# The first stage of a decoder layer: activations loaded channel-major and scaled by a row of rstd, instead of normalised and transposed

## The chip, the cores and the metric

The kernel runs on one core of one Trainium2 chip. The metric is the device time of one execution in microseconds (us), median of three runs; lower is better. Six queues of work matter: TensorE (PE, with its weight loads as PEld), VectorE (DVE), ScalarE (ACT), GpSimd (POOL), SyncE (SP), which issues nearly all loads, and the 16 DMA engines that carry them.

## The reference, cut to what matters

One layer: a normalised input is projected once for three token mixers, the mixers are merged, and a mixture of experts follows. The change touches only the two lines that begin it.

```
h    = rmsnorm(x, g_mix)                  # x (512, 1024): y = x * rsqrt(mean(x*x, -1) + eps) * g
proj = einsum('bsd,dc->bsc', h, w_in)
...
kv   = einsum('bmd,dc->bmc', rmsnorm(mem, g_mem), w_mem_kv)   # mem (256, 1024), w (1024, 1024)
k_m, v_m = split(kv, 2)
k_m  = rmsnorm(k_m per head, g_km)
```

## The kernel before, in words

Every fp32 product is made of three fast ones: each operand is split into a rounded high part and a rest, and `mm3` (L156 to L159) adds high by high, high by rest and rest by high. The split of a weight chunk is one cast on ACT (`wh`, L127) and one subtraction on DVE (`wl`, L128); that of an activation is one ACT instruction and one DVE instruction (`evac_split`, L153 and L154).

The first stage, "mem kv", does two things at once. It multiplies the memory tokens by the eight chunks of `w_mem_kv`, k = 0 to 7, each 128 rows of the contraction and 512 KB: per chunk two halves of tokens (m) by two halves of columns (n), so four groups of three products of 512 columns, twelve in all, summed over the chunks in four PSUM banks (`kvp`). And it makes `hh`/`hl`, the split and normalised x with channels on partitions, which all later projections read. For that x is loaded token-major in four tiles (L255), its squares are summed per token (L223 on ACT, L225 on DVE), `rsqrt` (L144) runs a scale on DVE and a power on POOL for each tile, DVE multiplies the tile by it in two halves (`xn`, L265), PE transposes 32 blocks of 128 by 128 (`transpose_x`, L248), and each of the eight results is split out of PSUM.

The order in which each engine works is fixed when the program is built: a scheduler lays out the instructions of each engine in one list, and the engine takes them in that order, each waiting for its inputs. SP issues the loads in list order too. The weight chunks go through a ring of three buffers (tag "w"), so the load of chunk k + 3 is issued only after the DVE split of chunk k. Behind the eight chunks come the first projections, "conv" (L330 on, products at L314), which need all of `hh` and `hl`; the scheduler puts the small transposes of the normalised keys `kn` (L301) among their first products.

Much later, in the stage "w_o", x is loaded once more, channel-major, from `xt` (L798), and the experts' weights are fetched ahead by SP (`fetch`, L772) into every buffer that the earlier stages give back.

Of the kernel before, what the change touches and what calls it, by code (L numbers as in the profile page):

```python
# [8 lines left out]
F32 = mybir.dt.float32  # L9
F32R = mybir.dt.float32r  # L10
# [10 lines left out]
P = 128  # L21
# [68 lines left out]
def build(nc, tc, I, O, dbg=None):  # L90
    V, A, G, T, SY = nc.vector, nc.scalar, nc.gpsimd, nc.tensor, nc.sync
    es = ExitStack()
    with es:
# [25 lines left out]
        tri16 = cpool.tile([P, 2 * P], BF16, name="tri16")  # L119
        nhalf = cpool.tile([P, 16], F32, name="nhalf")  # L120
        G.memset(nhalf, -0.5)

        def small(name, n, dt=F32, tag="small", bufs=16):
            return cpool.tile([P, n], dt, name=name, tag=tag, bufs=bufs)
# [57 lines left out]
        def h_pairs(name):  # L182

            hi, lo = [], []
            for k in range(KD):
                if k >= 3:
                    x2 = hp.tile([P, 1024], F32R, name=f"{name}{k}", tag="hw" if k < 6 else "hx", bufs=3 if k < 6 else 2)
                    hi.append(x2[:, 0:512])
                    lo.append(x2[:, 512:1024])
                    continue  # L190
                tags = ("xh", "xl") if k < 2 else ("th", "ah")
                hi.append(hp.tile([P, 512], F32R, name=f"{name}h{k}", tag=tags[0], bufs=2 if k < 2 else 1))
                lo.append(hp.tile([P, 512], F32R, name=f"{name}l{k}", tag=tags[1], bufs=2 if k < 2 else 1))
            return hi, lo
# [31 lines left out]


        mark("mem kv")
        kv_raw = [raw_w("kv", 0)]
        mx = [hp.tile([P, D], F32, name=f"m{i}", tag=("hx", "hw")[i // 2], bufs=2 + i // 2) for i in range(4)]  # L230
        SY.dma_start(mx[0], I["memt"][0])
        kv_raw.append(raw_w("kv", 1))
        SY.dma_start(mx[1], I["memt"][1])
        SY.dma_start(csg[:, 0:P], I["cst"][:, C_KEEP:C_KEEP + P])
        kv_raw.append(raw_w("kv", 2))
# [16 lines left out]
        xn, rm = [], []  # L252
        for k in range(KD):
            if k < NT:
                SY.dma_start(xt0[k], I["x"][k])  # L255
            elif k < NT + 2:
                SY.dma_start(mx[k - 2], I["mem"][k - NT])
            if k == 3:
                for t in range(NT):
                    ss = small("ss", 1)  # L260
                    sum_sq(ss, xt0[t], t != 1, "y")
                    rsqrt(ss, ss, 1.0 / D, EPS)
                    for i in range(2):
                        xn.append(g2("B", f"xn{t}{i}"))
# [3 lines left out]
            wh, wl = split_w(kv_raw[k] if k < RING else raw_w("kv", k))  # L268
            for m in range(2):
                o = (k % 2) * 256 + m * P  # L270
                ah, al = mh[k // 2][:, o:o + P], ml[k // 2][:, o:o + P]
                for n in range(2):
# [521 lines left out]
        x_v = I["xt"].rearrange("k p n -> p k n")  # L794
        X = []
        for c in range(KD // 2):
            xt = rp.tile([P, 2, S], F32, name=f"xr{c}", tag="xc", bufs=2)
            SY.dma_start(xt, x_v[:, 2 * c:2 * c + 2])  # L798
            X.append(xt)
        wo_raw = [raw_w("wo", c) for c in range(KD)]  # L800
        gB = eat("wg", "gB")
# [476 lines left out]
def layout(x, mem, g_mix, w_in, b_gate, g_qa, g_ka, g_idx_k, conv_w, conv_b, ln_g, ln_b, g_mem, w_mem_kv,  # L1278
# [45 lines left out]
    def row(a):  # L1324
# [11 lines left out]
    return dict(x=x.reshape(NT, P, D), xt=np.ascontiguousarray(x.T).reshape(KD, P, S), mem=mem.reshape(2, P, D),  # L1336
                memt=np.ascontiguousarray(mem.T.reshape(2, 4, P, 256).transpose(0, 2, 1, 3)).reshape(2, P, D), wp=wp, we=we, sm=sm,
                gf=f(g_ffn), cst=constants())

# [34 lines left out]
```

## Time and profile before

| | |
|---|---|
| median of 3 runs | 776.18 us (774.14 to 776.66) |
| profiled execution | 777.4 us, its span 775.6 us |
| PE busy | 714.2 us (92% of the span) |
| DVE, ACT, POOL busy | 478.5, 266.0, 94.8 us |
| loads and stores | 161.13 MB, mean 208 GB/s |

The span is what the profile's times are counted in; about 2 us of the execution lie around it. Busy shares are means over stages that have different limits, so the first 60 us, where the change lies, have to be read by themselves, in the timeline and in windows of 2 us.

### The profile page before, as it was taken

Reading aid. Unit: us, or ns where it says so; the run is one execution under the profiler, and the core shown is the slowest. Engines: PE = TensorE matmul, PEld = TensorE weight load, DVE = VectorE, ACT = ScalarE, POOL = GpSimd, SP = SyncE. Lnnn points to the kernel's source line nnn. Section 1 sums busy time; section 2 is a strip of 40 time slices with the busy share of each in tenths; the row PEclk is TensorE's granted clock in tenths of the full one; section 3 lists DMA queues with packets and bytes.
Section 4 is the critical chain, followed back from the end, with each engine's and each line's share of the span. In section 5 each row is a group of like instructions: output and inputs, shape, how many; then the busy total and the mean of one; then the engine's idle time right before and its main releaser. Section 6 shows DMA issues by size and latency. Waiting matters only on the chain. (4 is left out here: it accounts for less than half of the span.)

```text
span 775.6 us, 10017 instructions
## 1 busy us (share of the span) xinstructions
PE 714.2 (92%) x3434; PEld 477.7 (62%) x3434; DVE 478.5 (62%) x1086; ACT 266.0 (34%) x502; POOL 94.8 (12%) x82
## 2 busy tenths in 40 slices
PE   6999999999999999999998999749999999789882
PEld 4778888887878778887776888633333333233220
DVE  5879989999999999999985844371211212111100
ACT  6732255365632466246774322101111111000100
POOL 1010010022000140000000000121226421100011
PEclk9999999999999999999999999858999999999997
DMA  9632311213223223220314799958999999999982
GB/s 357 219 123 81 93 72 55 81 56 109 82 81 90 75 81 102 89 82 27 109 55 190 247 368 336 365 208 299 394 385 363 353 379 377 373 382 388 396 336 52
DMA packets 56684, 161.13 MB, mean 208 GB/s; under 512 B 9508, under 2 KB 17956, under 8 KB 56624
## 3 DMA queue, kind: packets, MB, share of 16 engines
q1 hardware_dynamic: 41264, 147.21, 51.7%
q0 software_dynamic: 6624, 8.46, 4.8%
q10 hardware_dynamic: 8736, 4.73, 2.0%
q8 instruction: 29, 0.48, 0.2%
q14 instruction: 31, 0.25, 0.1%
HBM read 162.93 MB, written 13.11 MB: 227 GB/s over the span
## 5 line engine op out<-in xcount | busy, mean ns | idle before, releaser
L1143 PE MATMUL up<-we,xt 128*64 128x512 f32 x544 | 142.2, 611 | 4.3 <-DMA we<-in_we 4.2
L127 ACT CAST wh<-w 128x1024 fp32r<-128x1024 f32 (+2 forms) x75 | 78.3, 1046 | 88.1 <-PE proj L314 22.4
L128 DVE TENSOR_TENSOR wl<-w,wh 128x1024 fp32r<-128x1024 f32 (+2 forms) x75 | 91.0, 1214 | 10.5 <-ACT wh L127 8.6
L1143 PEld LDWEIGHTS up<-we,xt 128*64 128x64 f32 x544 | 39.6, 139 | 80.0 <-issue 60.5
L328 DVE SCALAR_TENSOR_TENSOR y<-u,conv_wh,y 128x512 f32<-128x512 f32 x120 | 84.2, 745 | 0.3
L1133 DVE COPY y<-dn 128x512 f32<-128x512 f32 x17 | 11.8, 692 | 109.9 <-PE dn L1157 109.9
L1157 PE MATMUL dn<-we,acth 128*64 128x512 f32 x272 | 74.7, 610 | 0.8 <-issue 0.6
L314 PE MATMUL gate<-h,wh 128*128 128x512 f32 x240 | 67.8, 397 | 0.0
L1132 ACT COPY y<-dn 128x512 f32<-128x512 f32 x17 | 10.0, 586 | 123.6 <-PE dn L1157 70.0
L1157 PEld LDWEIGHTS dn<-we,acth 128*64 128x64 f32 x272 | 24.2, 139 | 44.9 <-issue 36.7
L314 PEld LDWEIGHTS gate<-h,wh 128*128 128x128 f32 x240 | 44.4, 188 | 9.6
L1134 POOL DMA_INDIRECT out<-y,midx x16 | 25.4, 1585 | 137.2 <-DVE y L1133 109.3
L314 PE MATMUL gate<-h,wl 128*128 128x512 f32 x120 | 34.6, 399 | 0.0
L314 PE MATMUL mm<-h,wh 128*128 128x512 f32 x120 | 32.7, 396 | 0.0
L1151 DVE COPY acth<-atr 128x256 f32<-128x256 f32 x17 | 7.2, 425 | 39.3 <-PE atr L1149 33.1
L1115 ACT COPY xt<-xtr 128x512 f32<-128x512 f32 x17 | 9.9, 584 | 61.0 <-PE xtr L1114 61.0
L422 ACT ACTIVATE gt<-gate,bgate 128x512 f32<-128x512 f32 x24 | 16.5, 686 | 39.7 <-PE gate L314 39.5
L1126 DVE SCALAR_TENSOR_TENSOR acts<-up,mwt,acts 128x256 f32<-128x256 f32 x16 | 7.7, 484 | 31.7 <-ACT acts L1125 30.2
L604 DVE MAX8 v<-score 128x8 f32<-128x256 f32 (+2 forms) x48 | 26.6, 558 | 0.8
L605 DVE MATCH_REPLACE8 score<-v,score 128x256 f32<-128x256 f32 (+2 forms) x48 | 26.0, 543 | 0.0
L314 PEld LDWEIGHTS gate<-h,wl 128*128 128x128 f32 x120 | 22.4, 187 | 5.5 <-issue 0.5
L314 PEld LDWEIGHTS mm<-h,wh 128*128 128x128 f32 x120 | 22.4, 187 | 5.2
(396 smaller groups left out, 1441.2 us busy)
## 6 DMA issues: line engine op xcount, KB each, us to landing
we<-in_we SPq DMA_DIRECT2D x192, 512.0 KB
w<-in_wp SPq DMA_DIRECT2D x75, 512.0 KB
x<-in_x SPq DMA_DIRECT2D x4, 512.0 KB
xr<-in_xt SPq DMA_DIRECT2D x4, 512.0 KB
out<-x1t ACTq DMA_DIRECT2D x8, 256.0 KB
h2d<-x1t ACTq DMA_DIRECT2D x8, 256.0 KB
m<-in_memt SPq DMA_DIRECT2D x2, 512.0 KB
m<-in_mem SPq DMA_DIRECT2D x2, 512.0 KB
```

Of the source, the lines that this page charges most:

```text
L127: A.copy(wh, w)
L128: V.tensor_sub(wl, w, wh.bitcast(F32))
L314: T.matmul(ps, a[:, k * P:(k + 1) * P], b[k], start=(a is wh and b is rh and k == 0), stop=(b is rl and k == n - 1))
L328: V.scalar_tensor_tensor(Y[c], U[c][:, j:j + S], w, Y[c], op0=ALU.mult, op1=ALU.add)
L422: A.activation(t, ps, AF.Tanh, scale=0.5, bias=bgate[:, b * 8 + c:b * 8 + c + 1])
L604: V.max(v8, sel[t])
L605: V.match_replace(sel[t], v8, sel[t], GONE)
L1132: A.copy(y[:, 0:512], yp[0])
L1133: V.tensor_copy(y[:, 512:1024], yp[1])
L1134: G.indirect_dma_start(out=O["out"], out_offset=bass.IndirectOffsetOnAxis(ap=ix[:, col:col + 1], axis=0), in_=y, in_offset=None, bounds_ch ...
L1143: T.matmul(ps[h * CAP:(h + 1) * CAP], xt[k // 4][:, o + h * CAP:o + (h + 1) * CAP], ws[h][:, i * 512:(i + 1) * 512], start=(k == 0), stop= ...
L1157: T.matmul(yp[n][h * CAP:(h + 1) * CAP], at[:, f * P + h * CAP:f * P + (h + 1) * CAP], ws[h][:, n * 512:(n + 1) * 512], start=(f == 0), st ...
```

## The change

`xt`, the channel-major copy of x that the host lays out, is stored as four contiguous blocks of two channel groups (so L798 now reads 4 KB in one piece per partition), and it is loaded in the first stage too, as eight tiles `xc` of 256 KB. The token-major x is still loaded, for the squares alone. The four columns of sums go through one `rsqrt`. PE then multiplies the broadcast column by the identity, four times, which gives one PSUM tile in which every partition holds the row of 512 factors; ACT copies it to SBUF (`rows`). Even tiles are multiplied by the row on DVE, which reads it from PSUM, odd tiles on POOL, which reads the copy. The eight splits then read `xc` in SBUF.

Beside that, ten products of a zeroed tile that nobody reads stand ahead of PE's work; chunk 0 and the first memory tile are loaded and split in halves; the loop over a chunk's products has columns outside and tokens inside; and the load of chunk 2 goes ahead of that of the constants.

```diff
+        warm = cpool.tile([P, P], F32, name="warm")
+        V.memset(warm, 0.0)
...
+        junk = trt()
+        for _ in range(10):
+            T.matmul(junk[:, 0:P], warm, warm, start=True, stop=True)
+        for i in range(2):
+            SY.dma_start(w0[:, i * 512:(i + 1) * 512], I["wp"][W_KEYS.index(("kv", 0)), :, i * 512:(i + 1) * 512])
+            SY.dma_start(mx[0][:, i * 512:(i + 1) * 512], I["memt"][0, :, i * 512:(i + 1) * 512])
...
-        def transpose_x():
+        xc = [g2("B", f"xc{k}") for k in range(KD)]
+        def norm_x():
+            row = trt()
+            for t in range(NT):
+                T.matmul(row[:, t * P:(t + 1) * P], rx[:, t:t + 1].to_broadcast([P, P]), ident, start=True, stop=True)
+            rows = g2("ms", "row")
+            A.copy(rows, row)
             for k in range(KD):
-                ps = (trt if k % 2 == 0 else sct)()
-                for t in range(NT):
-                    T.transpose(ps[:, t * P:(t + 1) * P], xn[2 * t + k // 4][:, (k % 4) * P:(k % 4 + 1) * P], ident)
-                evac_split(hh[k], hl[k], ps, Q["g_mix"][:, k:k + 1])
+                if k % 2:
+                    G.tensor_mul(xc[k], xc[k], rows)
+                else:
+                    V.tensor_mul(xc[k], xc[k], row)
+                evac_split(hh[k], hl[k], xc[k], Q["g_mix"][:, k:k + 1])
...
         for k in range(KD):
...
+            if 2 <= k < 6:
+                for i in range(2):
+                    n = 2 * (k - 2) + i
+                    SY.dma_start(xc[n], x_v[n // 2, :, i * 512:(i + 1) * 512])
             if k == 3:
                 for t in range(NT):
-                    ss = small("ss", 1)
-                    sum_sq(ss, xt0[t], t != 1, "y")
-                    rsqrt(ss, ss, 1.0 / D, EPS)
-                    for i in range(2):
-                        xn.append(g2("B", f"xn{t}{i}"))
-                        V.tensor_scalar_mul(xn[-1], xt0[t][:, i * 512:(i + 1) * 512], ss)
+                    sum_sq(rx[:, t:t + 1], xt0[t], t != 1, "y")
+                rsqrt(rx, rx, 1.0 / D, EPS)
             if k == 5:
-                transpose_x()
+                norm_x()
```

The lists that the scheduler makes differ from the start of the program to the first projection; after it they are the same on every engine. Three places matter. SP's list after the first chunks, before (w is a weight chunk, x a token-major tile, m_104 and m_105 the token-major memory):

```order
L255 DMA x_72<-in_x 128x1024
L255 DMA x_73<-in_x 128x1024
L132 DMA w<-in_wp 128x1024
L257 DMA m_104<-in_mem 128x1024
L132 DMA w<-in_wp 128x1024
L257 DMA m_105<-in_mem 128x1024
L132 DMA w<-in_wp 128x1024 x3
```

and with the change:

```order
L271 DMA x_72<-in_x 128x1024
L277 DMA xc_163<-in_xt 128x512
L277 DMA xc_164<-in_xt 128x512
L271 DMA x_73<-in_x 128x1024
L277 DMA xc_165<-in_xt 128x512
L277 DMA xc_166<-in_xt 128x512
L134 DMA w<-in_wp 128x1024
L273 DMA m_116<-in_mem 128x1024
L277 DMA xc_167<-in_xt 128x512
L277 DMA xc_168<-in_xt 128x512
L134 DMA w<-in_wp 128x1024
```

Two `xc` tiles now stand ahead of the last x tile, four ahead of chunk 3, six ahead of chunk 4 and eight ahead of chunk 5.

DVE's list from the split of chunk 4 to that of chunk 6, before (h_143 to h_147 are tiles 3 to 7 of the activations):

```order
L128 TENSOR_TENSOR wl<-w,wh 128x1024
L154 SCALAR_TENSOR_TENSOR h_143<-sc,sm,h_143 128x512
L145 TENSOR_SCALAR rm<-rm 128x1 x2
L154 SCALAR_TENSOR_TENSOR h_144<-tr,sm,h_144 128x512
L128 TENSOR_TENSOR wl<-w,wh 128x1024
L154 SCALAR_TENSOR_TENSOR h_145<-sc,sm,h_145 128x512
L154 SCALAR_TENSOR_TENSOR h_146<-tr,sm,h_146 128x512
L154 SCALAR_TENSOR_TENSOR h_147<-sc,sm,h_147 128x512
L128 TENSOR_TENSOR wl<-w,wh 128x1024 x2
```

and with the change (h_158 to h_162 are the same five tiles, xc_169 is tile 6):

```order
L130 TENSOR_TENSOR wl<-w,wh 128x1024
L156 SCALAR_TENSOR_TENSOR h_158<-xc_166,sm,h_158 128x512
L156 SCALAR_TENSOR_TENSOR h_159<-xc_167,sm,h_159 128x512
L264 TENSOR_TENSOR xc_169<-xc_169,tr 128x512
L156 SCALAR_TENSOR_TENSOR h_160<-xc_168,sm,h_160 128x512
L147 TENSOR_SCALAR rm<-rm 128x1 x2
L156 SCALAR_TENSOR_TENSOR h_161<-xc_169,sm,h_161 128x512
L156 SCALAR_TENSOR_TENSOR h_162<-xc_170,sm,h_162 128x512
L130 TENSOR_TENSOR wl<-w,wh 128x1024 x3
```

The split of chunk 5 stood between tiles 4 and 5 and stands behind all of them now.

POOL's list, before, from its first power to the keys':

```order
L146 TENSOR_TENSOR ss<-ss,nhalf 128x1 x4
L146 TENSOR_TENSOR rm<-rm,nhalf 128x1 x2
L146 TENSOR_TENSOR kss<-kss,nhalf 128x4 x2
L146 TENSOR_TENSOR rsm<-rsm,nhalf 128x4 x4
L146 TENSOR_TENSOR kss_1550<-kss_1550,nhalf 128x3
```

and with the change:

```order
L148 TENSOR_TENSOR rx<-rx,nhalf 128x4
L262 TENSOR_TENSOR xc_164<-xc_164,row 128x512
L262 TENSOR_TENSOR xc_166<-xc_166,row 128x512
L262 TENSOR_TENSOR xc_168<-xc_168,row 128x512
L262 TENSOR_TENSOR xc_170<-xc_170,row 128x512
L148 TENSOR_TENSOR rm<-rm,nhalf 128x1 x2
```

One power of four columns stands for four of one, and four products of 512 columns follow it.

## Rows read from the trace of the kernel before

**Rows 1.** Windows: PE, PEld, DVE, ACT, POOL busy (count), granted clock, DMA share, GB/s.
```profile
440.00:500.00 60.00, 58.75 (x313) 49.63 (x312) 24.80 (x37) 16.59 (x24) 1.92 (x2) 0.98 0.99 348
...
560.00:650.00 90.00, 89.30 (x446) 33.41 (x446) 17.19 (x31) 12.70 (x23) 31.78 (x28) 1.00 1.02 370
```
**Rows 2.** Chain that ended last: start, length, what.
```profile
742.06 12.44 DMA we<-in_we
```
**Rows 3.** Waits of SP's queue from 380 us on: total, times, longest.
```profile
SPq L798 <- PE pva L706: 0.3, 1, 0.3
```
**Rows 4.** Windows of the first stage, columns as in rows 1.
```profile
18.00:20.00 2.00, 0.77 (x5) 0.53 (x5) 1.15 (x4) 0.00 (x0) 0.70 (x2) 1.00 1.03 410
...
22.00:24.00 2.00, 2.00 (x7) 1.53 (x7) 1.79 (x3) 2.00 (x4) 0.00 (x0) 0.59 0.59 123
```
**Rows 5.** Timeline of PE: start, length, instruction, wait before it.
```profile
16.25 0.40 PE L159 MATMUL kv<-wh,ml 128*128 128x512 f32 x1
...
21.11 2.06 PE L157 MATMUL kv<-wh,mh 128*128 128x512 f32 x4
...
37.65 0.40 PE L158 MATMUL kv<-wl,mh 128*128 128x512 f32 x1
37.88 0.40 PE L159 MATMUL kv<-wh,ml 128*128 128x512 f32 x1
...
42.39 0.41 PE L301 MATMUL tr<-csg,kn 128*128 128x128 f32 x2 [0.59 <-DVE kn L293]
...
46.40 0.87 PE L301 MATMUL tr<-csg,kn 128*128 128x128 f32 x6 [0.56 <-DVE kn L293]
```
**Rows 6.** Timeline of ACT.
```profile
13.61 1.06 ACT L223 ACTIVATE junk<-x 128x1024 bf16<-128x1024 f32 x1 [0.98 <-DMA x<-in_x]
...
16.25 1.05 ACT L127 CAST wh<-w 128x1024 fp32r<-128x1024 f32 x1 [0.21 <-DMA w<-in_wp]
...
22.01 0.69 ACT L153 ACTIVATE hh<-tr,sm 128x512 fp32r<-128x512 f32 x1
22.58 0.70 ACT L153 ACTIVATE h<-sc,sm 128x512 fp32r<-128x512 f32 x1
```
**Rows 7.** Timeline of DVE.
```profile
20.59 1.22 DVE L128 TENSOR_TENSOR wl<-w,wh 128x1024 fp32r<-128x1024 f32 x1
...
22.39 0.74 DVE L154 SCALAR_TENSOR_TENSOR hl<-sc,sm,hh 128x512 fp32r<-128x512 f32 x1
23.05 0.75 DVE L154 SCALAR_TENSOR_TENSOR hl<-tr,sm,hh 128x512 fp32r<-128x512 f32 x1
...
28.43 1.23 DVE L128 TENSOR_TENSOR wl<-w,wh 128x1024 fp32r<-128x1024 f32 x1 [0.19 <-ACT wh L127]
...
41.57 0.68 DVE L293 TENSOR_TENSOR kn<-kv,kss 128x512 f32<-128x512 f32 x1
```
**Rows 8.** Timeline of POOL: three powers.
```profile
38.61 2.12 POOL L146 TENSOR_TENSOR kss<-kss,nhalf 128x4 f32<-128x4 f32 x1 [11.27 <-DVE kss L145]
44.33 1.02 POOL L146 TENSOR_TENSOR kss<-kss,nhalf 128x4 f32<-128x4 f32 x1 [3.60 <-DVE kss L145]
...
174.74 5.58 POOL L146 TENSOR_TENSOR kss<-kss,nhalf 128x3 f32<-128x3 f32 x1 [1.22 <-DVE kss L145]
```
**Rows 9.** Timeline of DVE beside the first and the last of these.
```profile
38.64 1.22 DVE L128 TENSOR_TENSOR wl<-w,wh 128x1024 fp32r<-128x1024 f32 x1
...
178.39 1.22 DVE L128 TENSOR_TENSOR wl<-w,wh 128x1024 fp32r<-128x1024 f32 x1
```
**Rows 10.** One line's instructions: shortest/median/longest ns, first and last start.
```profile
L651 PE MATMUL rs<-identr,rc x8: 275/275/373, 292.3 to 293.1; 128*128 128x128 f32 x8
```
**Rows 11.** Another line's: the longest plain POOL instruction.
```profile
L1098 POOL MEMSET xg<- x2: 952/953/954, 432.5 to 496.6; 128x1024 f32 x2
```
**Rows 12.** Groups by line on POOL: busy, mean ns, idle before.
```profile
L146 POOL TENSOR_TENSOR ss<-ss,nhalf 128x1 f32<-128x1 f32 x4 | 2.2, 562 | 16.4 <-DVE ss L145 16.4
```

More of the change, by code (lines that the diff above doesn't have):

```diff
@@ L228, in build @@
         mark("mem kv")
-        kv_raw = [raw_w("kv", 0)]
+        junk = trt()
+        for _ in range(10):
+            T.matmul(junk[:, 0:P], warm, warm, start=True, stop=True)
+        w0 = wpool.tile([P, 1024], F32, name="w", tag="w")
         mx = [hp.tile([P, D], F32, name=f"m{i}", tag=("hx", "hw")[i // 2], bufs=2 + i // 2) for i in range(4)]
-        SY.dma_start(mx[0], I["memt"][0])
-        kv_raw.append(raw_w("kv", 1))
+        for i in range(2):
+            SY.dma_start(w0[:, i * 512:(i + 1) * 512], I["wp"][W_KEYS.index(("kv", 0)), :, i * 512:(i + 1) * 512])
+            SY.dma_start(mx[0][:, i * 512:(i + 1) * 512], I["memt"][0, :, i * 512:(i + 1) * 512])
+        kv_raw = [w0, raw_w("kv", 1)]
         SY.dma_start(mx[1], I["memt"][1])
+        kv_raw.append(raw_w("kv", 2))
         SY.dma_start(csg[:, 0:P], I["cst"][:, C_KEEP:C_KEEP + P])
-        kv_raw.append(raw_w("kv", 2))
         mh = [g2("A", f"mh{k}", F32R) for k in range(4)]
@@ L242, in build @@
         hh, hl = h_pairs("h")
-        def transpose_x():
-            for k in range(KD):
-                ps = (trt if k % 2 == 0 else sct)()
-                for t in range(NT):
-                    T.transpose(ps[:, t * P:(t + 1) * P], xn[2 * t + k // 4][:, (k % 4) * P:(k % 4 + 1) * P], ident)
-                evac_split(hh[k], hl[k], ps, Q["g_mix"][:, k:k + 1])
+        x_v = I["xt"]
+        xc = [g2("B", f"xc{k}") for k in range(KD)]
[5 more added lines that the diff above has]
+            A.copy(rows, row)
+            for k in range(KD):
+                if k % 2:
[3 more added lines that the diff above has]
+                evac_split(hh[k], hl[k], xc[k], Q["g_mix"][:, k:k + 1])
         kvp = [[mmt("kv00"), mmt("kv01")], [mmt("kv10"), pvt("kv11")]]
-        xn, rm = [], []
+        rm, rx = [], small("rx", NT)
         for k in range(KD):
@@ L257, in build @@
                 SY.dma_start(mx[k - 2], I["mem"][k - NT])
+            if 2 <= k < 6:
+                for i in range(2):
+                    n = 2 * (k - 2) + i
+                    SY.dma_start(xc[n], x_v[n // 2, :, i * 512:(i + 1) * 512])
             if k == 3:
                 for t in range(NT):
-                    ss = small("ss", 1)
-                    sum_sq(ss, xt0[t], t != 1, "y")
-                    rsqrt(ss, ss, 1.0 / D, EPS)
-                    for i in range(2):
-                        xn.append(g2("B", f"xn{t}{i}"))
-                        V.tensor_scalar_mul(xn[-1], xt0[t][:, i * 512:(i + 1) * 512], ss)
-            if k == 5:
-                transpose_x()
[L268 to L272, printed above, removed]
+                    sum_sq(rx[:, t:t + 1], xt0[t], t != 1, "y")
+                rsqrt(rx, rx, 1.0 / D, EPS)
+            if k == 5:
+                norm_x()
+            if k == 0:
+                wh = spool.tile([P, 1024], F32R, name="wh", tag="wh")
+                wl = spool.tile([P, 1024], F32R, name="wl", tag="wl")
+                for i in range(2):
+                    split_into(wh[:, i * 512:(i + 1) * 512], wl[:, i * 512:(i + 1) * 512], w0[:, i * 512:(i + 1) * 512])
+            else:
+                wh, wl = split_w(kv_raw[k] if k < RING else raw_w("kv", k))
+            for n in range(2):
+                for m in range(2):
+                    o = (k % 2) * 256 + m * P
+                    ah, al = mh[k // 2][:, o:o + P], ml[k // 2][:, o:o + P]
                     mm3(kvp[m][n], ah, al, wh[:, n * 512:(n + 1) * 512], wl[:, n * 512:(n + 1) * 512],
@@ L792, in eat @@
             return ea.tile([P, 1024], dt, name=name, tag=tag, bufs=bufs)
-        x_v = I["xt"].rearrange("k p n -> p k n")
         X = []
@@ L797, in build @@
             xt = rp.tile([P, 2, S], F32, name=f"xr{c}", tag="xc", bufs=2)
-            SY.dma_start(xt, x_v[:, 2 * c:2 * c + 2])
+            SY.dma_start(xt.rearrange("p k n -> p (k n)"), x_v[c])
             X.append(xt)
@@ L1335, in layout @@
     x, mem = f(x)[0], f(mem)[0]
-    return dict(x=x.reshape(NT, P, D), xt=np.ascontiguousarray(x.T).reshape(KD, P, S), mem=mem.reshape(2, P, D),
+    return dict(x=x.reshape(NT, P, D), xt=np.ascontiguousarray(x.T.reshape(KD // 2, 2, P, S).transpose(0, 2, 1, 3)).reshape(KD // 2, P, 2 * S), mem=mem.reshape(2, P, D),
                 memt=np.ascontiguousarray(mem.T.reshape(2, 4, P, 256).transpose(0, 2, 1, 3)).reshape(2, P, D), wp=wp, we=we, sm=sm,
```

## The prediction

> **What bounds the kernel now.** I read the stage windows first. From 440 us on the DMA engines are full (share 0.99 at 348 GB/s, then 1.02 at 370) [rows 1], and the chain that ended last consists there of loads of experts' weights, the last one 12.44 us long [rows 2]. So the end is a stream of loads that runs from its start to the finish without slack. What starts it? SP's queue reaches the first load of that stage, L798, through a wait on PE's attention product [rows 3]. Whatever makes PE's earlier work late or early by some us therefore moves the stream, and the end, by about as much. Ahead of it I count the change as a shift of one point: the products of the first projection, behind which all lists are the same.
>
> The first stage has its own limits, seen in its windows and timelines. Until 20 us the DMA engines are full (1.03, 410 GB/s), and later not (0.59 of them, 123 GB/s) [rows 4]. PE ends chunk 2 at 16.65 us and starts chunk 3 at 21.11 [rows 5]: it sits between transposes that wait for normalised tiles, and its granted clock then reads 0.59 [rows 4], about the 1.2 GHz level of two. From there to 37.88 + 0.40 = **38.28 us**, where the last chunk's product ends [rows 5], PE is the bound: it has no wait in its rows, since the split of chunk 5 ends at 28.43 + 1.23 = 29.66 us on DVE [rows 7].
>
> The verdict can tell a change of about 0.3%, 2.3 us, from none.
>
> **The beginning: halves, unread products, loop order.** Chunk 0 and its tokens arrive in halves and PE starts earlier and, after the unread products, at a higher clock. I cost this at nothing: chunk 3 is what PE needs next, and its load ended the wait of ACT only at 16.25 us [rows 6], in a stretch of full DMA. What PE gains on chunks 0 to 2 it waits out before chunk 3. If that cover were gone, the start would be worth the time by which PE ends chunk 2 early, some 2 us. The later position of the constants hides likewise.
>
> **The loads.** Four `xc` tiles, 1.05 MB, now stand ahead of chunk 3. At 410 GB/s [rows 4] that is 2.6 us: chunk 3 lands at 16.25 + 2.6 = 18.8 us. The last x tile lay one 0.52 MB load behind the one that ended a wait at 13.61 [rows 6], so at 14.9; two `xc` tiles ahead of it make it 16.2. Chunks 4 and 5 each come with 1.57 MB, 3.8 us apart: 22.6 and 26.4.
>
> **The row.** Square 16.2 + 1.06 [rows 6]; 0.3 for two tiny instructions (an estimate, less than half of the 0.68 of a 512-column one [rows 7]); power of four columns 1.02 [rows 8]: 18.6 us. The four products of the row are eight passes that start 0.11 us apart [rows 10], 0.9 us, or twice that at the lower clock. PE will have had nothing to do since about 14.4, a longer pause than the one before the 0.59 of [rows 4], so I take 1.8: the row stands at 20.4, POOL's copy at 21.0 (ACT's 512-column instructions follow each other every 0.57 us [rows 6]).
>
> **DVE without trouble.** The split of chunk 3 ends at 18.8 + 1.05 + 1.22 = 21.1 [rows 6, 7]. Three products of `xc` at 0.6 each (priced by the 0.68-long row with a PSUM operand [rows 7], pipelined as the others are) make 22.9. ACT has one square of memory tokens, then three activations and the cast of chunk 4: about 1.2 + 3 x 0.57 + 1.05 from 21.0, 25.0. DVE then splits chunk 4 (1.14, the 1.22 row pipelined) and works off five tiles at 0.66 [rows 7] and one more `xc` at 0.6: 25.0 + 1.1 + 3.3 + 0.6 + 0.4 for small ones and hand-overs = 30.4. Only there, by the list, stands chunk 5: 31.6 us, against 29.66 before. PE then still has 8 products of chunk 5 and 24 of chunks 6 and 7. They start 37.88 - 37.65 = 0.23 us apart [rows 5]; 32 of them make 7.5 us, and the last ends at 39.1. So this term alone is **+0.8 us**, though 32 transposes (priced like the passes of [rows 10], 3.5 us) have left PE: before, they lay in the path; now PE waits instead.
>
> **POOL's four products.** No row has one, so I bound them. Streaming 1024 elements takes POOL 0.95 us [rows 11]; half of that, 0.5, is the lower end. From one column to four a power grows from 0.56 [rows 12] to 1.02 [rows 8], 0.15 us per column; at that slope 512 would be 76 us, the upper end, but a multiplication is no power. I take 1.3, nearest to the streaming row, for 1,024 elements read and 512 written. By the Trainium skill (GPSIMD Engine Reference, section 3.1) a two-input add of 2048 fp32 columns takes 4497 ns, which as an estimate is 1.1 us here; the sum would be some 0.2 us smaller.
>
> More matters whether they run at all. A power of four columns that takes 1.02 us beside a quiet DVE took 2.12 when DVE ran a split of 1.22 beside it [rows 8, 9]; and one of three columns took 5.58, from 174.74 to 180.32, beside an unbroken row of two-operand DVE instructions, the last of which ended at 179.61 [rows 8, 9]. DVE's rows there kept their 1.22. So POOL does not get to its operands while DVE reads two from SBUF. That now holds for every activation split too: `xc` and `hh` both lie in SBUF, where before one operand was PSUM. The first POOL product runs beside DVE's three PSUM-fed ones. The second is shut out until DVE has ended chunk 4's split at 26.3 and runs dry; it needs about 1.0 more, and ACT's tile, 0.69 [rows 6], follows: DVE goes on at 28.0, 1.7 late. The third and fourth use the gaps, for another 0.3. I take **+2.0 us**, PE ending at 41.1; lower end 0 (no shutting out), upper end 3.9 (three of the four wholly on the path).
>
> The Trainium skill (SBUF, State Buffer, section Who interferes with whom) calls this an exclusive lock of a shared port pair, where whoever starts first holds it for its whole instruction. The first half agrees with [rows 8, 9]. By it DVE should wait too when POOL is first; no row before shows that. The sum would be about the same, as then the hl tiles wait instead of the POOL products.
>
> **The keys.** The transposes of `kn` came after 13 conv products, now after 9, with the second group ten later; before, they made PE wait 0.59 and 0.56 [rows 5]. Four products fewer are 0.9 us less cover, against keys that end some 0.7 us sooner inside the last chunk by the new loop order, and POOL's power among more splits. I take **+0.5 us**, from 0 to 1.2.
>
> **Edits that cost nothing.** One rsqrt for four tiles and the missing `xn` are counted above. The 4 KB pieces of the late x load stay hidden in a stream that reads at full rate [rows 1].
>
> **The sum:** 0.8 + 2.0 + 0.5 = +3.3 us. Of the profiled execution's 777.4 that is 780.7; of the median 776.2 (the profiled one was 1.2 us above it) it is **779.5 us**.
>
> **Rivals.**
> Not slower: POOL's products slip into DVE's hand-overs, which the 1.02 row [rows 8] allows and the 5.58 row speaks against. Then +0.8 + 0.5 = +1.3: 777.5. It decides whether chunk 5's split ends before 32.5.
> Hidden: the lateness is absorbed before the expert stream, if that stream begins by a buffer that is given back for another reason than PE's products. The wait of 0.3 us is short [rows 3], which leaves room. Then 776.2.
> Faster: PE stays the bound as before, and the 16 transposes that stood behind chunk 3 (1.8 us) and 0.5 us of chunk 3 are saved: -2.3, 773.9. It needs chunk 5's split by 28.5 us. DVE's work in front of it, from 19.9 on, is 3 splits at 1.14, 4 products at 0.6 and 8 tiles at 0.66: 31.1 at the earliest by my prices, so these would have to be 25% too high.
> Slower still: PE pauses over 4 us ahead of chunk 5 and its clock falls a second time as in [rows 4]. Some 3 us at half the rate, partly covered by the wait for the split, cost another 1.3: 780.8; with POOL's upper end, 782.7.
> That the change does not do what it says concerns the unread products: PE idles after chunk 2 anyway, so their clock is lost again; that is in my sum.
>
> **Chances.** Shutting out, with or without the second fall: 0.50, slower. Slower still with POOL's products dearer: 0.05. Slip-in: 0.22 and hidden: 0.10, within 0.3%. Faster 0.13. From 775.2, about the lower third of what lies between faster and no change, to 781.8, between the two slower cases: some 0.1 lies beyond each end.
>
> **What would show it.** Right: PE's rows of the row products at 18 to 21 us; POOL's second product over 2 us long, or DVE's tiles beside it longer than 0.75; PE's wait ahead of chunk 5 over 3 us; the last chunk ending at 40 to 42 us instead of 38.28; the expert stream later by as much. Wrong: chunk 3 cast before 18 us (the loads did not queue up), POOL's products all near 1.3 with DVE unbroken (no shutting out), or the last chunk before 38 us; and if the end does not move with that point, the first paragraph is wrong.

## The result, and the profile after

The changed kernel takes **783.97 us** (median of 6 runs, 782.28 to 787.29) against 776.62 us for the kernel before on the same chip (6 runs): a ratio of 1.0100, 95% interval 1.0075 to 1.0126, some 7.4 us slower. The direction was forecast; the time lies above the range of 775.2 to 781.8. The profiled execution took 784.4 us, its span is 782.6 us against 775.6.

The answers to [rows 6], ACT's timeline of the changed kernel (start, length, instruction, the wait ahead of it and its releaser):

```profile
15.38 1.06 ACT L225 ACTIVATE junk<-x 128x1024 bf16<-128x1024 f32 x1 [1.43 <-DMA x<-in_x]
...
18.02 1.06 ACT L225 ACTIVATE junk<-x 128x1024 bf16<-128x1024 f32 x1 [1.49 <-DMA x<-in_x]
...
20.72 1.04 ACT L129 CAST wh<-w 128x1024 fp32r<-128x1024 f32 x1 [1.55 <-DMA w<-in_wp]
...
32.96 1.33 ACT L155 ACTIVATE h<-xc,sm 128x512 fp32r<-128x512 f32 x2 [2.72 <-DVE xc L264]
34.20 2.93 ACT L129 CAST wh<-w 128x1024 fp32r<-128x1024 f32 x3
```

x2 (the third token-major x tile), with no `xc` tile ahead of it, comes at 15.38 instead of 13.61, so 1.8 us are lost before the first additional load. The last x tile and the cast of chunk 3 (20.72 against 16.25) follow, with the two and four `xc` tiles that stand ahead of them. The last two lines are the wait for a product of DVE and, behind it, the cast of chunk 5 (34.20, before 27.36).

PE, to be held against [rows 5]:

```profile
20.62 2.07 PE L257 MATMUL tr<-csg,rx 128*128 128x128 f32 x8 [4.37 <-POOL rx L148]
...
27.20 1.20 PE L159 MATMUL kv<-wh,mh 128*128 128x512 f32 x4 [1.20 <-ACT wh L129]
...
31.06 0.80 PE L160 MATMUL kv<-wl,mh 128*128 128x512 f32 x1 [2.66 <-DVE wl L130]
...
35.28 1.20 PE L159 MATMUL kv<-wh,mh 128*128 128x512 f32 x4 [0.81 <-ACT wh L129]
...
43.88 0.40 PE L161 MATMUL kv<-wh,ml 128*128 128x512 f32 x1
45.87 0.51 PE L336 MATMUL mm<-hh,wh 128*128 128x512 f32 x1 [1.59 <-DVE vml L156]
```

The last memory product ends at 43.88 + 0.40 = 44.28 us, 6.0 us later than before. The first product of the convolution, which this text uses as its point of measurement from here on, starts at 45.87; in the kernel before it stood at 38.51, behind a wait of 0.23. That is 7.36 us, of which the new wait on `vml`, the split of the first memory values, makes 1.36.

DVE's and POOL's timelines, against [rows 7, 8], and one line's instructions with their shortest, median and longest ns:

```profile
23.35 1.88 DVE L264 TENSOR_TENSOR xc<-xc,tr 128x512 f32<-128x512 f32 x3 [0.33 <-ACT row L259]
25.15 4.72 DVE L156 SCALAR_TENSOR_TENSOR hl<-xc,sm,hh 128x512 fp32r<-128x512 f32 x3
29.79 1.21 DVE L130 TENSOR_TENSOR wl<-w,wh 128x1024 fp32r<-128x1024 f32 x1
...
35.27 3.50 DVE L130 TENSOR_TENSOR wl<-w,wh 128x1024 fp32r<-128x1024 f32 x3
```
```profile
23.40 5.92 POOL L262 TENSOR_TENSOR xc<-xc,row 128x512 f32<-128x512 f32 x4 [2.83 <-ACT row L259]
```
```profile
L156 DVE SCALAR_TENSOR_TENSOR hl<-xc,sm,hh x3: 1353/1758/1759, 25.2 to 28.1; 128x512 fp32r<-128x512 f32 x3
```

POOL was not shut out. Its four products run one behind the other from 23.40 to 29.32, and the three DVE splits beside them take 1.35 to 1.76 us each, where such a split took 0.74 [rows 7]. The split of chunk 4 stands behind them, and PE waits for it, 2.66 us. Windows, with the columns of [rows 1]:

```profile
22.00:24.00 2.00, 2.00 (x9) 1.71 (x8) 1.67 (x3) 1.26 (x2) 0.60 (x1) 0.58 1.02 402
...
30.00:32.00 2.00, 0.94 (x2) 0.84 (x3) 2.00 (x3) 0.24 (x1) 0.00 (x0) 0.62 0.00 0
32.00:34.00 2.00, 2.00 (x6) 1.55 (x5) 2.00 (x6) 1.04 (x2) 0.27 (x1) 0.52 0.89 277
```

After that wait the granted clock falls a second time, to 0.62 and 0.52, close to the 1.2 GHz level. Even so PE is through chunk 4 before chunk 5 is cast: it waits another 0.81 us for that cast and starts chunk 5 at 35.28, where the kernel before started it at 29.62. SP issues the first load of experts' weights at 421.20 us instead of 415.83, and the span ends 7.0 us later.

### The profile page after: what moved, and what is told of

Its sections match the earlier page's. It is cut to its first block, busy times and chain, and to the rows that moved or that the text cites. A ratio compares the mean times of both kernels' runs of the same rounds, so it can differ in the third digit from the quotient of the medians.

```text
span 782.6 us, 10017 instructions
## 1 busy us (share of the span) xinstructions
PE 716.6 (92%) x3430; PEld 479.3 (61%) x3430; DVE 480.6 (61%) x1081; ACT 266.6 (34%) x504; POOL 94.1 (12%) x83
## 5 line engine op out<-in xcount | busy, mean ns | idle before, releaser
L444 ACT ACTIVATE gt<-gate,bgate 128x512 f32<-128x512 f32 x24 | 16.5, 686 | 39.8 <-PE gate L336 39.5
```

The source lines that it names most:

```text
L444: A.activation(t, ps, AF.Tanh, scale=0.5, bias=bgate[:, b * 8 + c:b * 8 + c + 1])
```

## The experiments

All ratios are to the kernel before, on the same chip and in the same rounds. "Last product" is the end of the last memory product, "convolution" the start of its first product with the wait ahead of it; both, and the cast of chunk 3, are from each run's one profile. In e6 and e8 that cast stands behind other work in ACT's list, so there it does not time the load.

| kernel | ratio (95% interval) | cast of chunk 3 | last product | convolution (wait) |
|---|---|---|---|---|
| before | 1 | 16.25 | 38.28 | 38.51 (0.23) |
| changed | 1.0100 (1.0075 to 1.0126) | 20.72 | 44.28 | 45.87 (1.59) |
| e1_whole | 1.0102 (1.0063 to 1.0141) | 19.10 | 42.43 | 44.02 (1.60) |
| e2_all_dve | 1.0082 (1.0056 to 1.0107) | 19.90 | 42.62 | 44.67 (2.05) |
| e3_m_outside | 1.0079 (1.0057 to 1.0101) | 19.95 | 44.50 | 46.09 (1.59) |
| e4_no_unread | 1.0108 (1.0085 to 1.0131) | 20.33 | 43.83 | 45.43 (1.59) |
| e5_start_only | 1.0048 (1.0030 to 1.0065) | 17.96 | 39.41 | 41.13 (1.73) |
| e6_row_only | 1.0093 (1.0056 to 1.0130) | 20.43 | 43.73 | 45.11 (1.38) |
| e7_xc_late | 1.0076 (1.0049 to 1.0102) | 16.76 | 44.84 | 45.70 (0.86) |
| e8_one_x | 1.0146 (1.0110 to 1.0181) | 20.37 | 54.93 | 55.89 (0.97) |
| e9_x_once | 1.0038 (1.0024 to 1.0053) | 16.27 | 38.44 | 40.39 (1.95) |
| e10_narrow | 1.0053 (1.0033 to 1.0072) | 19.00 | 38.47 | 39.93 (1.47) |
| e11_start_whole | 1.0026 (1.0007 to 1.0044) | 16.29 | 37.30 | 39.12 (1.81) |
| e12_tiles_late | 1.0077 (1.0051 to 1.0103) | 18.96 | 41.91 | 43.50 (1.59) |
| e13_unread_only | 1.0012 (0.9997 to 1.0027) | 16.35 | 38.22 | 38.44 (0.23) |
| e14_n_outside | 1.0034 (1.0021 to 1.0047) | 17.00 | 40.12 | 41.85 (1.73) |

### The start edits

**e1_whole**: the first loads whole again, the rest as changed.

```diff
-        for i in range(2):
-            SY.dma_start(w0[:, i * 512:(i + 1) * 512], ...)
-            SY.dma_start(mx[0][:, i * 512:(i + 1) * 512], ...)
+        SY.dma_start(w0, I["wp"][W_KEYS.index(("kv", 0))])
+        SY.dma_start(mx[0], I["memt"][0])
```


> The changed kernel with chunk 0 and the first memory tile loaded whole again, still split in halves. Theory H (the half loads carry the opening of the stream at 240 to 320 GB/s in place of 404 to 426, and make all later loads 1.8 us late): ACT's wait for the third x tile ends at 13.6 us in place of 15.38, chunk 3 is cast at 18.9 in place of 20.72, the last product of chunk 7 ends at 42.5 in place of 44.28, the time falls by 1.8 us against the change's 784.0. Rival U (the unread products at PE's start slow the loads) and rival N (something else in the opening): none of these moves, 784.0.

**e4_no_unread**: the changed kernel without `warm` and its ten products.

> The changed kernel without the ten unread products. Theory H and the account that PE waits out its lead before chunk 3: the loads stay late (third x tile at 15.4 us), chunks 0 to 2 end up to 2 us later, still before the row products at 20.6, the end of chunk 7 and the time are unchanged within 0.5 us. Rival U (they slow the loads): the third x tile at 13.6 us and the time 1.8 us lower.

**e5_start_only** and **e11_start_whole**: the kernel before with all start edits, and with all of them but the half loads.

> The kernel before with the start edits alone (first chunk and first memory tile in half loads, chunk 0's split in halves, ten unread products, products of the memory keys and values with the columns outside); transposes, token-major normalising and loads of x as before. Theory H (the half loads make everything behind them in the queue late by 1.5 to 1.8 us): the square of x2 waits until 15.0 to 15.4 (before 13.61), chunk 3's cast until about 18 (16.25); the convolution starts about 1.5 us later than before (40 against 38.51), and the time is 1 to 2 us above the kernel before. Rival S (the opening is swallowed: the memory products wait for the splits anyway, as the prediction said): last memory product at 38.3 to 38.7, the convolution within 0.4 us of before, no difference in time.

> The kernel before with the start edits but without the half loads: ten unread products, products with the columns outside, chunk 0's split in halves; transposes and loads as before. Theory H (what the start edits cost, 3.7 us in the run with all of them, is the half loads): x2's square at 13.6 and chunk 3's cast at 16.3 as before, the convolution's start within 0.7 us of 38.51, time within 1 us of the kernel before. Rival V (part of it is the order of DVE's list at the end, where the split of the first values came to stand behind one of a convolution weight): PE still waits 1.6 to 1.8 us ahead of the convolution, which starts at 39.5 to 40, and the time is 1 to 2 us above the kernel before.

Measured: with whole loads the profile of e1 moves as expected, 1.6 us at chunk 3 and 1.85 at the convolution, but the ratio does not (1.0102 against 1.0100, uncertain by some 0.4 and 0.25%). On the old transposes the half loads again cost 2.11 us in the last product (39.41 against 37.30). In ratios that is 1.0048 against 1.0026, and those intervals overlap: the lateness is shown in the profiles, its worth in the time is not. e4 leaves the opening slow, so the unread products do not cause it (x2 is squared at 15.00, with whole loads in e1 at 13.76). Windows of 4 us of e5_start_only, then of e11_start_whole:

```profile
2.00:6.00 4.00, 4.00 (x23) 3.79 (x22) 1.50 (x3) 1.99 (x4) 0.00 (x0) 1.00 0.93 254
6.00:10.00 4.00, 1.68 (x7) 0.78 (x6) 1.77 (x4) 2.39 (x5) 0.00 (x0) 1.00 0.98 391
```
```profile
2.00:6.00 4.00, 3.23 (x18) 3.04 (x16) 0.69 (x1) 1.25 (x3) 0.00 (x0) 1.00 0.94 343
6.00:10.00 4.00, 3.57 (x13) 2.34 (x14) 3.36 (x6) 4.00 (x9) 0.00 (x0) 1.00 1.03 411
```

With halves the engines are as busy (0.93 and 0.94 of their time) but move 254 GB/s instead of 343. One profile of an opening is not exact: the square of x2 comes at 14.56 to 15.38 in the five kernels with half loads, and at 13.52 to 14.37 in the ten with whole ones that have that square; the means are 14.97 and 13.76, 1.2 us apart.

### The row form

**e6_row_only**: the kernel before with the other part of the change alone.

> The other part alone: x read channel-major and scaled by a row, half of the row products on POOL, with the loads of the opening whole, no unread products, chunk 0's split whole, the tokens outside as before. Theory H+P (late loads of chunk 3 by the channel-major tiles, 2.6 us, and DVE blocked behind POOL, 2.5 us, with the second clock fall): chunk 3's cast at about 18.9, three DVE splits of the tiles together at 4.6 us instead of 2.25, chunk 5's split not before 32, the convolution's start at 44 (as the run with whole loads, 44.02), time 4.5 to 6 above the kernel before. Rival O (the start edits and the order of the memory products are what costs, together more than singly): the convolution at 40 to 41 and no more than 2.5 us above the kernel before.

**e9_x_once**: as e1_whole, with `xc` loaded into the places of x; nothing is loaded twice, and the sums of squares run over other values.

```diff
-                SY.dma_start(xt0[k], I["x"][k])
+                SY.dma_start(xt0[k], x_v[k])
...
-        xc = [g2("B", f"xc{k}") for k in range(KD)]
+        xc = [xt0[k // 2][:, (k % 2) * 512:(k % 2 + 1) * 512] for k in range(KD)]
```


> The changed kernel with whole loads, and the channel-major tiles loaded in place of the token-major ones, so that the opening moves the bytes of the kernel before; the sums of squares are taken over these tiles and so over the wrong axis (same instructions, other values). Theory D (DVE is the bound from the row on: eight products and eight splits that could not begin before the row, 12 us, and five weight splits, 6 us, with the waits behind POOL): loads matter only up to the row; chunk 3's cast at 16.4 instead of 19.1, the row 1.5 to 2.5 us earlier, DVE's last chunk split at 34.5 to 35 instead of 36.6, the convolution's start at 42 to 42.5 (44.02 with whole loads, 38.51 before), time some 2 us under the run with whole loads. Rival H (the loads ahead of chunk 3 are most of it): the convolution's start at 39.5 or earlier and within 1.5 us of the kernel before.

**e10_narrow**: as e1_whole, the products nearly taken away.

```diff
-                if k % 2:
-                    G.tensor_mul(xc[k], xc[k], rows)
-                else:
-                    V.tensor_mul(xc[k], xc[k], row)
+                V.tensor_mul(xc[k][:, 0:8], xc[k][:, 0:8], row[:, 504:512])
```


> The changed kernel with whole loads, and the row product of each tile cut to eight of its 512 columns, all on DVE, without the copy of the row; every wait on the row stays, but about 5 us of products and all of POOL's are gone, so the tiles are left unscaled but for those columns. Theory D (DVE is the bound, its list is as long as what stands in it): the three splits of the first tiles at 0.75 each, the last chunk's split ends 4.5 to 6 us earlier than 36.6, the convolution starts at 39 to 40, time 777 to 778.5. Rival H (the loads ahead of chunk 3 and chunk 5's late load bind): chunk 5's load lands at 24 to 25 in either kernel, PE waits for it, the convolution not before 42 and the time over 780.

Measured: the row form alone is a ratio of 1.0093, nearly that of the whole change, though the start edits alone make 1.0048: the parts do not add. From the kernel before to e6, which differ by the row form alone, the last product moves from 38.28 to 43.73, by 5.45 us. From e11 to e1, which differ by it too, it moves from 37.30 to 42.43, by **5.13 us**. Without the second load of x, 3.99 us of that go (38.44); without the products, 3.96 (38.47). So in these profiles either part alone leaves some 1.15 us over e11 and both together 5.13. The ratios point the same way: 1.0038 and 1.0053 against 1.0102. A caution on e11: its profiled execution took 776.44 us, 3 us under its median, and its clock reads 1.00 from 20 to 24 us, where the kernel before has 0.57. Neither theory was right throughout: H put e9's convolution at 39.5 or earlier, D at 42 or later, and it came at 40.39; e10's convolution fits D and goes against H, but its median of 780.69 us is above D's 777 to 778.5.

What joins the two parts stands in the lists of DVE and ACT. DVE, ACT and PE of e1_whole:

```profile
20.18 1.23 DVE L130 TENSOR_TENSOR wl<-w,wh 128x1024 fp32r<-128x1024 f32 x1 [2.42 <-ACT wh L129]
...
23.12 4.61 DVE L156 SCALAR_TENSOR_TENSOR hl<-xc,sm,hh 128x512 fp32r<-128x512 f32 x3
...
30.11 0.67 DVE L263 TENSOR_TENSOR xc<-xc,tr 128x512 f32<-128x512 f32 x1
...
33.12 3.50 DVE L130 TENSOR_TENSOR wl<-w,wh 128x1024 fp32r<-128x1024 f32 x3
```
```profile
30.82 1.34 ACT L155 ACTIVATE h<-xc,sm 128x512 fp32r<-128x512 f32 x2 [2.80 <-DVE xc L263]
32.06 2.92 ACT L129 CAST wh<-w 128x1024 fp32r<-128x1024 f32 x3
```
```profile
28.91 0.79 PE L160 MATMUL kv<-wl,mh 128*128 128x512 f32 x1 [2.75 <-DVE wl L130]
...
33.14 1.82 PE L159 MATMUL kv<-wh,mh 128*128 128x512 f32 x4 [0.45 <-ACT wh L129]
```

The same in e10_narrow, where chunk 3 is as late (19.00) and chunk 5's split stands behind all tiles as well:

```profile
21.54 2.07 DVE L156 SCALAR_TENSOR_TENSOR hl<-xc,sm,hh 128x512 fp32r<-128x512 f32 x3
```
```profile
28.40 3.01 ACT L129 CAST wh<-w 128x1024 fp32r<-128x1024 f32 x3
```
```profile
25.51 1.20 PE L159 MATMUL kv<-wh,mh 128*128 128x512 f32 x4 [0.81 <-ACT wh L129]
...
29.48 1.21 PE L159 MATMUL kv<-wh,mh 128*128 128x512 f32 x4 [0.59 <-ACT wh L129]
```

In e1 DVE begins its list with the split of chunk 3, as soon as that is cast, and works without a gap from 20.18 to about 33. The three splits beside POOL take 4.61 us instead of 2.07. Behind them stand the split of chunk 4, for which PE waits 2.75, and the product of tile 6, for which ACT waits 2.80 before it can go on to cast chunk 5. PE starts chunk 5 at 33.14, in e10 at 29.48: that is 3.66 of the 3.96 us. So the late load sets when DVE's list begins, and the products and POOL how long it is. In e9 the list begins 2.83 us earlier (17.35), but DVE then waits 0.76 and 2.08 us, for the copy of the row and for ACT's tile, while POOL's products run: its list has gaps there. In e9 the scheduler also put chunk 5's split ahead of the last three tiles; what that order is worth, and what the missing loads, no run here separates.

PE's clock falls in e1's pause too, and not in e10 at that point. Windows of e1_whole, then of e10_narrow:

```profile
28.00:30.00 2.00, 1.09 (x3) 0.90 (x4) 2.00 (x3) 0.02 (x1) 0.00 (x0) 0.50 0.13 27
30.00:32.00 2.00, 2.00 (x6) 1.58 (x5) 2.00 (x6) 1.18 (x2) 0.41 (x1) 0.50 0.84 286
32.00:34.00 2.00, 1.55 (x4) 0.77 (x3) 1.87 (x3) 2.00 (x4) 0.74 (x2) 0.50 0.94 363
```
```profile
20.00:22.00 2.00, 1.97 (x6) 1.40 (x6) 1.90 (x6) 1.74 (x4) 0.00 (x0) 0.56 1.05 407
22.00:24.00 2.00, 2.00 (x7) 1.59 (x6) 1.88 (x7) 2.00 (x5) 0.10 (x1) 0.59 1.02 396
...
28.00:30.00 2.00, 1.41 (x6) 0.85 (x5) 1.91 (x4) 2.00 (x3) 0.00 (x0) 1.00 0.89 357
```

That fall is not what joins them. At half the rate PE still ends chunk 4 before chunk 5 is cast, and waits another 0.45 us. From the start of chunk 5 to the last product e1 takes 9.29 us, against 8.99 in e10, at full clock, and 9.00 in the changed kernel: some 0.3 us for the clock in e1, nothing in the changed kernel. And e10 and e9 have a fall of their own (0.50 in e9 from 20 to 22 us), at a place where e1 reads 1.00. A fall costs where PE waits for nothing behind it: in e6 it comes after the start of chunk 5 (33.13), products take 0.63 us instead of 0.40, and the stretch to the last product is 10.60 us.

```profile
36.56 0.63 PE L159 MATMUL kv<-wh,ml 128*128 128x512 f32 x1
```

In e9 POOL's products start at 19.38, while DVE waits for ACT's tiles, and DVE's `hl` splits come after them:

```profile
19.38 5.49 POOL L261 TENSOR_TENSOR x<-x,row 128x512 f32<-128x512 f32 x4 [1.92 <-ACT row L258]
```
```profile
25.87 2.06 DVE L156 SCALAR_TENSOR_TENSOR hl<-x,sm,hh 128x512 fp32r<-128x512 f32 x3
```

Three in 2.06 us, against 4.72 in the changed kernel with POOL beside them: the lengthening is the neighbour's, not the SBUF operands'.

**e2_all_dve**: the changed kernel with all eight products on DVE, without the copy of the row.

> The changed kernel with all eight products of x by the row on DVE, from PSUM, and no copy of the row for POOL. Theory P (a POOL product that started first holds DVE's splits of xc off until it ends: 4.72 us for three in place of 2.1): DVE's splits of the tiles all take 0.75 us, chunk 4's split ends near 28 us in place of 31.0, PE's clock does not fall a second time, and the last product of chunk 7 ends 2 to 3 us earlier, at 41 to 42, although DVE has 2.4 us more work; time 781 to 782. Rival D (DVE is simply full): the 2.4 us are added, the last product at 45 to 46.5, time 785 to 786.

Every split is back at 0.75 us, but four more products stand on DVE and the scheduler puts chunk 3's split behind the first two, which wait 3.36 us for their tile; the last product ends at 42.62, with an opening 0.8 us earlier than in the changed kernel. The ratio, 1.0082, cannot be told from 1.0100. Neither expectation held: P had the last product at 41 to 42, D at 45 or later. What the blocking cost, DVE's own products about cost again.

**e7_xc_late**: `xc` loads behind chunks 3 and 4.

```diff
-            if 2 <= k < 6:
-                ...
+                raw = kv_raw[k] if k < RING else raw_w("kv", k)
+                if 3 <= k < 5:
+                    for n in range(4 * (k - 3), 4 * (k - 3) + 4):
+                        SY.dma_start(xc[n], ...)
```


> The changed kernel with whole loads in the opening and the channel-major tiles asked for behind chunk 3 (0 to 3) and chunk 4 (4 to 7); arithmetic and POOL's share unchanged. Theory H (the place of the channel-major loads in the queue costs its 2.6 us one for one): x3's square at about 15.1 and chunk 3's cast at 16.4 (run with whole loads 16.40 and 19.10), row products from about 17.5 instead of 19.0, chunk 5's split about 2 us earlier than 33, the convolution's start at 42 (44.02), the time 2 us under the changed kernel with whole loads: about 781. Rival D (two megabytes more must land before the last tile whatever the order; the last channel-major tile lands near 24 either way, and DVE's list with POOL's products sets the end): the convolution's start within 0.6 us of 44.0.

Chunk 3 is cast at 16.76, 2.3 us earlier than in e1, and the convolution comes no earlier (45.70 against 44.02; the ratios, 1.0076 and 1.0102, cannot be told apart). Neither H nor D had that. PE now waits in one piece for chunk 5, whose cast stands behind tiles that come last. Here the clock falls behind the start of chunk 5 (33.72): the windows from 32 to 40 us read 0.54 and 0.61, and the stretch to the last product takes 11.12 us.

```profile
33.72 2.08 PE L159 MATMUL kv<-wh,mh 128*128 128x512 f32 x4 [5.17 <-ACT wh L129]
```

**e12_tiles_late**: `if k == 7` for `if k == 5` ahead of `norm_x()`.

> The changed kernel with whole loads, and the row with its products and tile splits written ahead of chunk 7 instead of chunk 5, so that the splits of chunks 5 and 6 go ahead where DVE's list can take them. Theory D (the sum of DVE's list is the bound, its order only says who waits): PE's wait for chunk 5 shrinks, but the work behind is the same; the convolution's start within 1 us of 44.02. Rival O (the order is the bound: chunk 5's split behind all tiles): chunk 5's split by 30, the last memory product at 38 to 40, the convolution at 41 to 42, 2 us faster than the run with whole loads.

Inconclusive: the scheduler moved chunk 5's split ahead of one tile only (its cast starts at 31.84), PE still waits 2.66 us for chunk 4, and the convolution comes at 43.50. That is within D's range, but O's order was never there to be tested.

### The wait ahead of the convolution

**e3_m_outside**: the changed kernel with the old order of the loop.

> The changed kernel with the loop over a chunk's products as before, tokens outside and columns inside. Theory L (the new loop order ends the value columns last, and the first projection waits for their PSUM buffer): PE's wait ahead of the first projection, 1.59 us, goes back to 0.2 to 0.5, the time falls by 1.1 to 1.4 us. Rival (that wait follows from late DVE work, whatever the order): still 1.2 or more, time unchanged.

**e13_unread_only** and **e14_n_outside**: the kernel before with one start edit each.

```diff
-            for m in range(2):
+            for n in range(2):
...
-                for n in range(2):
+                for m in range(2):
```


> The kernel before with the ten unread products alone: whole loads, tokens outside, whole split of chunk 0, transposes. Theory V (the wait ahead of the convolution comes from the order with the columns outside): the wait is 0.2 to 0.4 us as before, the last memory product ends at 37.2 to 38.3, the convolution starts between 37.5 and 38.5, time 0 to 1 us under the kernel before. Rival W (it comes from the unread products, which bring the memory products forward of the work on DVE): a wait of 1.4 us or more, the convolution at 38.7 or later, time no better than before.

> The kernel before with the order of the memory products alone, columns outside. Theory V: the first values end some 0.7 us later inside the last chunk and their split stands behind one of a convolution weight (1.22 us) in DVE's list; the wait ahead of the convolution is 1.4 to 1.9 us, the convolution starts at 39.7 to 40.2 (38.51 before), the time is 1 to 1.5 us above. Rival W: wait 0.2 to 0.4, the convolution at 38.5, no difference in time.

DVE of e13_unread_only, then of e14_n_outside:

```profile
36.93 0.69 DVE L296 TENSOR_REDUCE kss<-ksq 128x4 f32<-128x512 f32 x1
37.64 0.75 DVE L156 SCALAR_TENSOR_TENSOR vml<-kv,rm,vmh 128x512 fp32r<-128x512 f32 x1
```
```profile
38.84 0.69 DVE L290 TENSOR_REDUCE kss<-ksq 128x4 f32<-128x512 f32 x1 [0.24 <-ACT ksq L287]
...
39.64 0.17 DVE L145 TENSOR_SCALAR kss<-kss 128x4 f32<-128x4 f32 x1
...
39.91 1.22 DVE L128 TENSOR_TENSOR wl<-w,wh 128x1024 fp32r<-128x1024 f32 x1
41.05 0.74 DVE L154 SCALAR_TENSOR_TENSOR vml<-kv,rm,vmh 128x512 fp32r<-128x512 f32 x1
```

With the old transposes the loop order decides: columns outside, the first values (`kv01`) are complete later within the last chunk, the scheduler puts the split of a convolution weight ahead of theirs, and PE waits 1.73 us instead of 0.23. That alone is a ratio of 1.0034, 2.6 us; this profile also has an opening 0.76 us later than before, so the 41.85 is not the order's alone. In the changed kernel the old order does not help: in e3 a weight's split stands ahead of `vml` all the same, and the wait is 1.59; in e6, which has the old order too, it is 1.38.

### A version to beat both

**e8_one_x**: x read once, channel-major; sums by products of its squares with a column of ones; DVE alone multiplies.

```diff
+                    for t in range(NT):
+                        T.matmul(sx[:, KD * t + n:KD * t + n + 1], sq[:, t * P:(t + 1) * P], one, start=True, stop=True)
```


> A version meant to beat both: x is read only once in this stage, channel-major, in place of the token-major tiles; the sums of squares come from squares of the channel-major tiles (six on ACT, two on DVE) and products of one column with ones; the row is scaled in on DVE alone; whole loads, no unread products, tokens outside. Theory H+P (the two megabytes ahead of chunk 3 and POOL's lock are what the change loses): chunk 3's cast at 16.3 as before, chunk 5's load at 20 to 21, DVE's splits of the tiles 0.75 each, the convolution's start at 38 to 40, time 776 to 779, at or under the kernel before. Rival C (the row form itself is the slow part, since no tile can be split before the last token tile's sum has come: the transposes began with the row already applied): row products not before 20.5, the last chunk's split not before 36, convolution's start 42 or later, and over 3 us above the kernel before.

```profile
16.12 10.44 PE L275 MATMUL tr<-one,sqx 128*128 128x1 f32 x64
```

It failed: the 32 products of one column are 64 passes that take PE 10.4 us, with the clock at 0.50 from 20 us on, and the products of the row start at 29.08 us instead of 20.62. Of all versions only e13, the unread products alone, is not slower than the kernel before, and it is not faster either (0.9997 to 1.0027). None beats both.

## Why the prediction was right or wrong

**That a late first projection moves the end by as much: right.** 7.36 us at the convolution, 7.0 in the span, 7.4 in the medians. The first load of experts' weights is only 5.4 us later; where between these points the rest went and came back was not followed.

**"The loads" and "The row": right, on an opening that was itself late.** With whole loads the last x tile is squared at 16.40 (16.2 forecast), chunk 3 cast at 19.10 (18.8), and the row stands at 19.01 + 1.16 = 20.17 (20.4); in the changed kernel each is 1.6 us or more later.

**"The beginning": a step that failed.** I costed halves, unread products and loop order at nothing, because chunk 3's load covers what PE gains. I never asked whether the halves make the loads behind them late. They did in the profiles, by 1.85 us in the last product (changed against e1); in the time this does not show (1.0100 against 1.0102). The loop order, which I saw only in the keys, took the first values' split out of its place (e14, 1.0034). Together the start edits alone cost 0.48% (0.30 to 0.65).

**The row form: the path right, the sum too small.** It was forecast at +3.3 us in all, the keys included; alone (e6) it costs 0.93% (0.56 to 1.30), some 7.2 us (4.3 to 10.1). So this is the step that takes the time out of the forecast range: on top of it the start edits add 0.76 us at the convolution (45.11 to 45.87) and nothing that the ratios show (1.0093 to 1.0100). The path was the one that I described: chunk 5's split stands behind all tiles in DVE's list, and PE waits for chunk 5, though the releaser that its row names is the chunk's cast on ACT, which waits for the product of tile 6 in the same list. I had that split end at 33.6 (31.6 and the 2.0 for POOL); in e1 it ended at 33.12 + 1.22 = 34.3, in e6 0.1 later. What I had too short lies behind it: 7.5 us to PE's last product, against 8.1 in e1 and 9.3 in e6, and a wait ahead of the convolution that grew by more than 1.1 us in both.

**"POOL's four products": the size nearly right, the direction half of it.** I let DVE shut POOL out, from rows in which DVE was there first: these two instructions of the kernel before were running when the powers of [rows 8] began at 38.61 and 174.74.

```profile
38.44 0.28 DVE L215 TENSOR_TENSOR tq<-csg,sm 128x128 f32<-128x128 f32 x1
...
174.57 1.22 DVE L128 TENSOR_TENSOR wl<-w,wh 128x1024 fp32r<-128x1024 f32 x1
```

Here POOL came first (its products start at 23.40, the splits at 25.15), and DVE waited: 4.72 us for three splits that take 2.06 without a neighbour, 2.7 us against my +2.0. The Trainium skill (SBUF, State Buffer, section Who interferes with whom) says that whoever starts first holds the ports for its whole instruction, and the run with and without POOL beside the splits agrees. A POOL product took 1.30 to 1.72 us, around the 1.3 that I took; by the Trainium skill's add (GPSIMD Engine Reference, section 3.1) the estimate was 1.1.

**"Slower still": the rival's number was met by luck.** My sum had PE's last product at 41.1, and 42.4 with the 1.3 us of that rival; e1, with whole loads, ended at 42.43. But the second fall of the clock, which came ahead of chunk 4 and not chunk 5, cost e1 about 0.3 us: PE had to wait for chunk 5's cast anyway. The rest is 0.7 us by which chunk 5's split ended late, and about 0.3 that I had too short behind it. Where the fall comes behind the start of chunk 5, as in e6, it costs 1.6 us (10.60 against 8.99). I priced it without asking what PE waits for next.

**"The keys": wrong wait.** Forecast +0.5 ahead of the transposes of `kn`; those waits made 0.70 us in all, against 0.59 + 0.56 before [rows 5]. What grew was the wait one step earlier, on `vml`, by 1.36 us.

The steps at the convolution, by pairs of profiles: unread products and order without halves -0.98 (before to e11), row form +5.13 (e11 to e1), half loads +1.85 (e1 to changed), the wait on `vml` +1.36; sum +7.36. The forecast had 0, +2.8, 0 and +0.5. The first and third rest on single profiles of about a microsecond's scatter, and the parts depend on their order: by way of e6 the row form makes +6.60 and the start edits +0.76. What stays open is why half loads are slow in the opening, and why the parts do not add.

## What to carry to other kernels

A load that is asked for twice and an engine that is asked to help can each fit into the slack and still not fit together: look for the list in which both delays meet (here DVE's, whose beginning the loads set and whose length the products set), and ask whether it still has a gap. Before pricing a fall of the clock, ask what the engine waits for next; if that comes late anyway, the slower work ahead of it is covered. When work moves to GpSimd beside VectorE, ask which of them starts first, since that one's whole instruction is what the other waits for. An edit that only reorders products is not free where a scheduler sets the lists: look at what now stands ahead of the first result that the next stage reads.

## What the runs showed of the hardware

Loads of half rows (2 KB of each partition) at the very start moved 254 GB/s from 2 to 6 us (e5), against 343 with whole rows (e11), with the same share of busy engines; in the changed kernel it was 281, in e1 363. Yet the `xc` tiles, halves of the same shape in the middle of the stage, came at about 400 (402 at 22 to 24 us). It is the place or the neighbours and not the shape alone, and no run here says which. A DVE split was lengthened by a POOL product, from 0.74 to 1.76 us; the rows of before had shown it the other way round only [rows 8, 9]. Whether ten unread products ahead of the work help the clock later, these runs do not say: from 20 to 24 us it read 0.57 with them in e13, as in the kernel before, and 1.00 in e1 and e11, which have them, and in e4, which does not.
